# One diffusion step on one core: partial sums of the down projection kept in DRAM, some weight halves loaded by casting DMAs, and a new placement of the side work

## The chip, the cores and the metric

The kernel runs on one core of one Trainium2 chip, in one launch. The metric is the device time in microseconds (us). The program of before took 1320.09 us (median of three runs, 1320.08 to 1320.2).

## What is computed

One layer of a hybrid transformer acts on 128 context tokens and 128 latent tokens with the same fp32 weights (D = 2048, feed-forward width 8192):

```
m = silu(cond) @ w_ada + b_ada            # 6 vectors of 2048 per stream: shift, scale, gate, twice
h = rms_norm(x) * (1 + scale1) + shift1
p = h @ w_in                              # 8704 columns: q, k, v of mixers A and B, gate_A, gate_B
o_A = windowed attention (sink, rotary), o_B = neighbourhood attention (bias)
x = x + gate1 * ((sigmoid(gate_A) * (o_A @ w_br_a) + sigmoid(gate_B) * (o_B @ w_br_b)) @ w_out)
h2 = rms_norm(x) * (1 + scale2) + shift2
x = x + gate2 * (relu(h2 @ w_up) ** 2 @ w_down)
```

The two streams differ in `cond` and in the attention. Outputs are both streams and the new keys and values of the context.

## The kernel before

**Steps.** All big products run as 456 steps in a list (`wsteps`). A step is one 128x1024 fp32 weight tile (512 KB). SyncE loads it (`raw`), ScalarE copies it to fp32r (`wH`, through `copy`, L101), VectorE subtracts to get the rest (`wL`, L249), and TensorE does twelve 512-column matmuls: two k rows, two streams, and three products (high by high, low by high, high by low). Steps 0 to 135 are the input projection, 136 to 167 the branches, 168 to 199 the output projection, 200 to 215 the first two blocks of the up projection. Then for p = 1 to 7 come 16 steps of an up pair (216 to 231, 248 to 263, ...) and 16 of a down piece (232 to 247, ...); 440 to 455 are the last down piece.

**Order.** Nothing is scheduled by a tool: each engine's order is the order in which Python emits. `run` walks the steps. Before step i it emits the loads that are due up to i + `RUN[i]` (a load's due time is its step less 4), then the preparation (`prep_to`) of the steps up to i + `LOOK[i]`, then the step's matmuls, then what `at(i, ...)` has hung behind it. So a digit of `LOOK` moves a ScalarE and a VectorE instruction past their neighbours, and a digit of `RUN` moves loads past what else SyncE issues. `POST` gives three steps for each q/k unit: square sums (`qk_stat`, whose `rsqrt` runs on GpSimd), scaling (`qk_apply`, ScalarE and VectorE, which needs GpSimd's answer `rq`) and transposes (`qk_T`). `JOBS` gives five steps for each of eight attention jobs: scores, softmax, normalise, transposes, values. `DOTS*` place the modulation dot products on VectorE (`dot`, L1448, two of 1.2 us for each job).

**Low halves by DMA.** For the steps in `LO_DMA`, `lo_dma` has ScalarE write -`wH` (L255) and GpSimd issue an accumulating DMA of the fp32 weights onto it (L256), so VectorE does nothing.

**Up pairs.** `up_pair` treats a pair of 512-column blocks at eight k positions. At the positions in `FAST` it uses seven products in place of eight (a Winograd form): 21 matmuls in place of 24, with sums of weights made on VectorE and ScalarE (`prep_x`, `prep_y`). There are 34 such groups.

**Down pieces.** `down_unit(p, n)` multiplies 1024 of the 8192 hidden values into one of four 512-column blocks. The running sum of each block stays in SBUF (`dsum`, four of the 50 tiles of the pool `gen`). ScalarE copies it into two PSUM banks ahead of a unit (`seed`, `SEED_AT` = 3 steps before, or at the end of an up pair) and out again behind it.

**Modulation columns.** `mod_pair` takes two 128-column blocks (512 KB quarters `araw`, L308) at the steps in `ADA_AT`; `pair_mm` does the two blocks one after the other, 256 columns at a time in four 32-column groups of TensorE (L316). For the dot products the SiLU of `cond` is needed as a row over all partitions: `load_cond` broadcasts `crow`, `silu_cond` applies SiLU to the whole 128x1024 tile (ScalarE L1426, VectorE L1427) and GpSimd stores one row (L1429) for later use. This happens four times.

Of the kernel before, what the change touches and what calls it, by code (L numbers as in the profile page):

```python
# [51 lines left out]
LO_DMA = [50, 54, 56, 63, 77, 107, 129, 141, 145, 176, 184, 187, 188, 189, 203, 228, 233, 250, 286, 297, 360, 388, 392, 403, 447]  # L52
LO_AHEAD = 2

LOOK = "744424025212231324035524333325102425654224523344556654121016645555652437464478555443415652626353315000022636320000411134313532054023400446230326565645456443574337324421522555644666674052000205311111322534110323455554321045445111013410444324654734331001335565775443654453304436533423355423455542233213213545587654334232213213202440122544412433432313432443523324313211333435533333213331314344422557756822145342656433332302254541454475574464555546763333345544"
RUN = "788542236756223234111350006888532114464200022565595544354324444434399864356664356543323535443143130021224242014401314413432357530331035587886464765545676867644543555342013141268665576965588956265287998988511453877787785653022200123446553345324545104653232464345673321110102222521121211202355533232133432223443232410110000000011234344212022112531112752123301000112323643331133410100122454235566436675432012021222210010001154457832224556577677636445664422234"
CONST_AT = [83, 81]
XL_DMA = []
ADA_AT = [None, 4, 13, 22, 25]
XS_AT = {1: 3, 2: 24, 3: 34}  # L60
POST = {('kvA', 0): [81, 83, 89], ('qA', 0): [84, 84, 92], ('qA', 1): [86, 88, 92], ('kB', 0): [90, 94, 98], ('qB', 0): [94, 98, 104], ('kB', 1): [98, 101, 103], ('qB', 1): [102, 105, 107]}
JOBS = [[93, 94, 95, 100, 106], [93, 94, 98, 104, 106], [98, 98, 100, 106, 114], [101, 104, 107, 110, 111], [107, 107, 110, 115, 120], [109, 109, 111, 118, 121], [113, 114, 115, 126, 128], [116, 116, 119, 122, 124]]
# [3 lines left out]
DOTS = [44, 58, 61, 61, 62, 63, 65, 66, 66, 66, 69, 70, 71, 71, 72, 74, 76, 81, 84, 85, 89, 91, 94, 96, 96, 98, 100, 100, 101, 102, 102, 105, 107, 107, 107, 110, 110, 111, 113, 114, 115, 117, 117, 117, 120, 120, 120, 121, 121, 123, 123, 124, 127, 128, 128, 132, 132, 133, 133, 134, 135, 136, 141, 143, 144, 144, 149, 151, 151, 152, 157, 157, 157, 162, 163, 170, 172, 174, 174, 175, 176, 176, 178, 179, 179, 182, 183, 190]  # L66
DOTS2 = [224, 231, 231, 233, 235, 237, 238, 242, 245, 263, 265, 269, 275, 296, 299, 304, 309, 329, 331, 331, 333, 333, 353, 360, 362, 364, 366, 368, 382, 391, 394, 396]
STAT_AT = [-1, -1, 8, 16]
T_PAIR = [[9, 10], [6, 9], [8, 9], [8, 9], [10, 14], [10, 10], [11, 14]]
P_PAIR = [[5, 5], [2, 2], [2, 4], [6, 2], [4, 2], [4, 4], [6, 0]]  # L70
M_TE = (3,)
M_AT = [6, 6, 9]
# [7 lines left out]
def tile_hybrid_step(ctx: ExitStack, tc: tile.TileContext, a):  # L80
# [7 lines left out]

    act, dve, pe, pool, sync = nc.scalar, nc.vector, nc.tensor, nc.gpsimd, nc.sync
# [80 lines left out]

    r = SM(2, "r")
# [69 lines left out]
    def prep(st):  # L241
# [8 lines left out]
        st.pop("raw")  # L250
# [18 lines left out]

    by_dma = sorted(LO_DMA)  # L270

    def run():
        loads.sort(key=lambda x: x[:2])
        for st in wsteps:
# [6 lines left out]
            while by_dma and by_dma[0] < to + LO_AHEAD:  # L281
                prep_to(by_dma[0] - LO_AHEAD)
                lo_dma(wsteps[by_dma.pop(0)])
# [35 lines left out]
    def pair_mm(box, j, fb):  # L319
        for q in range(4):  # L320
            pair_mm_q(box, j, fb, q)
# [172 lines left out]
    def mod_pair(f):  # L494
# [3 lines left out]
        for j in range(2):  # L498
            load_at(i, lambda j=j: pair_load(box, 0, k0 + j))
            at(i, lambda j=j: pair_mm(box, j, k0 + j))  # L500
# [22 lines left out]
    def begin():  # L523
# [42 lines left out]
        mod_q(0, 3)  # L566
        x_scale(0, 0, 2)
# [61 lines left out]
    dp = ctx.enter_context(tc.tile_pool(name="dram", bufs=1, space=bass.MemoryType.DRAM))  # L629
# [584 lines left out]
    def up_pair(p):  # L1214
# [32 lines left out]
        for pos, is_fast in enumerate(kinds):  # L1247
# [16 lines left out]
            def prep_x(b=b, pos=pos):  # L1264
                b["XH"] = G("XH", F32R)
                copy(b["XH"], b["x"]["raw"])
                if 8 * p + pos in XL_DMA:
                    b["XL"] = G("XL", F32R)
                    minus_plus(b["XL"], b["XH"], b["x"]["src"])
# [28 lines left out]
            def mm_y(st, b=b, j=j, pos=pos, end=end):  # L1298
# [37 lines left out]
            for i, (nm, pf, mf) in enumerate((("x", prep_x, mm_x), ("y", prep_y, mm_y))):  # L1336
                add_step(a["w_upF"][p - 1, j, i], mf, key)
                b[nm] = wsteps[-1]
                wsteps[-1]["prep"] = pf

    dsum = {}
# [10 lines left out]
    def seed(p, n):  # L1352

        seeds[p, n] = [bank("acc", pacc) for _ in range(2)]
        for s in range(2):
            copy(seeds[p, n][s], dsum[n][:, s, :])
        if p == last:
            dsum.pop(n)

    def down_unit(p, n):  # L1360
        def evac(acc):
            if p == 0:
                dsum[n] = G(f"dsum{n}").rearrange("p (s n) -> p s n", s=2)
            if p == last:
                out_s(acc, n, range(2))
                return
            for s in range(2):
                copy(dsum[n][:, s, :], acc[s])
# [8 lines left out]
        if p and (n or p == last):  # L1377
# [4 lines left out]
        unit(a["w_down"], 512 * n, [4 * j for j in PIECES[p]], stat, evac, ("down", p, n), seeded if p else None)  # L1382
# [31 lines left out]
    silu_row = {}  # L1414

    def load_cond(h, tag):
        for s in range(2):
            cB[s, tag] = G(f"cB{s}")
            src = silu_row[s, h] if (s, h) in silu_row else a["crow"][s:s + 1, 1024 * h:1024 * h + 1024]
            sync.dma_start(cB[s, tag], src.partition_broadcast(P))  # L1420

    def silu_cond(h, s, tag):
        if (s, h) in silu_row:
            return
        t, c = G("sgB"), cB[s, tag]
        act.activation(t, c, AF.Sigmoid)  # L1426
        dve.tensor_tensor(c, c, t, op=OP.mult)  # L1427
        silu_row[s, h] = dp.tile([1, 1024], F32, name=f"silu{s}{h}")
        pool.dma_start(silu_row[s, h], c[0:1, :])  # L1429
# [52 lines left out]
    def dots(jobs, name):  # L1482
# [147 lines left out]
```

## Time and profile before

| | |
|---|---|
| median of three runs | 1320.09 us |
| the profiled execution | 1319.34 us, of it 1317.6 us from the first to the last instruction |
| mean granted TensorE clock | 0.999 |
| TensorE (PE) busy | 1300.7 us, 99% |
| VectorE (DVE) busy | 1149.5 us, 87% |
| ScalarE (ACT) busy | 925.8 us, 70% |
| GpSimd (POOL) busy | 62.9 us, 5% |
| DMA | 393.81 MB, 299 GB/s on average |

PEld is TensorE's weight load, SP is SyncE, L12 is line 12 of the kernel. The records of matmuls overlap, so that a busy TensorE says that work was queued; the idle time is the better guide, and where it lies.

### The profile page before, as it was taken

Reading aid. Unit: us, or ns where it says so; the run is one execution under the profiler, and the core shown is the slowest. Engines: PE = TensorE matmul, PEld = TensorE weight load, DVE = VectorE, ACT = ScalarE, POOL = GpSimd, SP = SyncE. Lnnn points to the kernel's source line nnn. Section 1 sums busy time; section 2 is a strip of 40 time slices with the busy share of each in tenths; the row PEclk is TensorE's granted clock in tenths of the full one; section 3 lists DMA queues with packets and bytes.
Section 4 is the critical chain, followed back from the end, with each engine's and each line's share of the span. In section 5 each row is a group of like instructions: output and inputs, shape, how many; then the busy total and the mean of one; then the engine's idle time right before and its main releaser. Section 6 shows DMA issues by size and latency. Waiting matters only on the chain.

```text
span 1317.6 us, 17782 instructions
## 1 busy us (share of the span) xinstructions
PE 1300.7 (99%) x6137; PEld 1056.9 (80%) x6137; DVE 1149.5 (87%) x1530; ACT 925.8 (70%) x1310; POOL 62.9 (5%) x71
## 2 busy tenths in 40 slices
PE   8999999999999999999999999999999999999998
PEld 4777888878777878888888888888888888888886
DVE  4569999999999999999779999897989998979753
ACT  5667766679866555755687867969678687796881
POOL 0000000241100000000000000000000000000000
PEclk9999999999999999999999999999999999999999
DMA  9999999887889999999498865888587696857692
GB/s 376 406 389 409 383 363 322 318 301 294 291 332 383 400 380 335 370 352 368 146 322 290 273 229 185 278 285 286 196 301 237 208 319 242 298 162 298 201 348 80
DMA packets 148394, 393.81 MB, mean 299 GB/s; under 512 B 51792, under 2 KB 52752, under 8 KB 148304
## 3 DMA queue, kind: packets, MB, share of 16 engines
q1 hardware_dynamic: 144016, 378.16, 78.4%
q0 software_dynamic: 4144, 14.44, 5.5%
q8 instruction: 48, 0.79, 0.2%
q14 instruction: 42, 0.34, 0.1%
q10 hardware_dynamic: 144, 0.08, 0.0%
HBM read 373.97 MB, written 8.70 MB: 290 GB/s over the span
## 4 chain that ended last, share of the span: by engine, by line
PE 63%; DVE 4%; issue 1%; DVEq 0%
PE acc L300 12%; PE acc L299 12%; PE acc L301 12%; PE Q L1225 6%; PE Q L1226 6%; PE Q L1224 6%; DVE wL L249 1%; DVE junk L1448 1%; DVE aT L1448 1%; PE Z L1225 1%; PE Z L1226 1%; PE Z L1224 1%; PE acc L1063 1%; PE acc L1044 1%; PE acc L1061 1%
## 5 line engine op out<-in xcount | busy, mean ns | idle before, releaser
L249 DVE TENSOR_TENSOR wL<-raw,wH 128x1024 fp32r<-128x1024 f32 x360 | 425.1, 1225 | 73.2 <-ACT wH L101 72.3
L101 ACT ACTIVATE wH<-raw 128x1024 fp32r<-128x1024 f32 (+1 forms) x391 | 388.6, 1044 | 71.9 <-PE acc L300 13.0
L1448 DVE SCALAR_TENSOR_TENSOR aT<-aT,cB 128x1024 f32<-128x1024 f32 x144 | 173.6, 1221 | 1.1
L1448 DVE SCALAR_TENSOR_TENSOR junk<-aT,cB 128x1024 bf16<-128x1024 f32 x144 | 173.9, 1224 | 0.0
L417 PE MATMUL acc<-wH,hH 128*128 128x512 f32 x276 | 109.1, 395 | 0.0
L419 PE MATMUL acc<-wH,hL 128*128 128x512 f32 x276 | 107.9, 391 | 0.0
L418 PE MATMUL acc<-wL,hH 128*128 128x512 f32 x276 | 107.9, 391 | 0.0
L101 ACT ACTIVATE uH<-raw 128x1024 fp32r<-128x1024 f32 x34 | 36.2, 1064 | 66.4 <-DVE raw L1286 60.7
L417 PEld LDWEIGHTS acc<-wH,hH 128*128 128x128 f32 x276 | 52.2, 189 | 13.1 <-issue 1.4
L419 PEld LDWEIGHTS acc<-wH,hL 128*128 128x128 f32 x276 | 52.1, 189 | 11.0
L418 PEld LDWEIGHTS acc<-wL,hH 128*128 128x128 f32 x276 | 52.3, 189 | 10.5
L101 ACT ACTIVATE tH<-t 128x1024 fp32r<-128x1024 f32 x34 | 36.0, 1059 | 29.8 <-DVE t L1279 28.8
L299 PE MATMUL acc<-wH,hH 128*128 128x512 f32 x128 | 52.2, 408 | 0.0
L300 PE MATMUL acc<-wL,hH 128*128 128x512 f32 x128 | 50.3, 393 | 1.7 <-DVE wL L249 1.7
L452 PE MATMUL acc<-wH,hH 128*128 128x512 f32 x128 | 50.5, 394 | 1.1 <-ACT acc L101 1.1
L453 PE MATMUL acc<-wL,hH 128*128 128x512 f32 x128 | 49.9, 390 | 0.3 <-DVE wL L249 0.3
L301 PE MATMUL acc<-wH,hL 128*128 128x512 f32 x128 | 50.0, 390 | 0.0
L454 PE MATMUL acc<-wH,hL 128*128 128x512 f32 x128 | 49.9, 390 | 0.0
L1289 DVE TENSOR_TENSOR uL<-raw,uH 128x1024 fp32r<-128x1024 f32 x34 | 41.7, 1226 | 1.2
L1279 DVE TENSOR_TENSOR t<-raw 128x1024 f32<-128x1024 f32 x34 | 41.5, 1219 | 1.3 <-PE Q L1225 1.3
L101 ACT ACTIVATE acc<-dsum 128x512 f32<-128x512 f32 x56 | 31.7, 589 | 14.7 <-DVE t L1010 7.3
L1288 DVE TENSOR_TENSOR tL<-t,tH 128x1024 fp32r<-128x1024 f32 x34 | 41.4, 1219 | 0.0
(643 smaller groups left out, 3353.7 us busy)
## 6 DMA issues: line engine op xcount, KB each, us to landing
raw<-in_w_in SPq DMA_DIRECT2D x133, 512.0 KB, 8.0
raw<-in_w_down SPq DMA_DIRECT2D x128, 512.0 KB, 5.9
aT<-in_w_adaT SPq DMA_DIRECT2D x80, 512.0 KB, 8.7
raw<-in_w_upF SPq DMA_DIRECT2D x68, 512.0 KB, 5.4
aT<-in_w_gT SPq DMA_DIRECT2D x64, 512.0 KB, 6.9
raw<-in_w_up SPq DMA_DIRECT2D x60, 512.0 KB, 6.1
araw<-in_w_pair SPq DMA_DIRECT2D x48, 512.0 KB, 9.5
raw<-in_w_out SPq DMA_DIRECT2D x32, 512.0 KB, 9.8
```

What stands on the lines that cost most here:

```text
L101: act.activation(out, in_, AF.Copy)
L249: dve.tensor_tensor(st["lo"], st["raw"], st["hi"].bitcast(F32), op=OP.subtract)
L299: pe.matmul(acc[tb], sh, wh[:, k, :], start=f, stop=False, skip_group_check=seeded)
L300: pe.matmul(acc[tb], sh, wl[:, k, :], start=False, stop=False, skip_group_check=seeded)
L301: pe.matmul(acc[tb], sl, wh[:, k, :], start=False, stop=l, skip_group_check=seeded)
L417: pe.matmul(acc[tb], sh, wh[:, k, :], start=opened[u] and k == 0, stop=False, skip_group_check=skip)
L418: pe.matmul(acc[tb], sh, wl[:, k, :], start=False, stop=False, skip_group_check=skip)
L419: pe.matmul(acc[tb], sl, wh[:, k, :], start=False, stop=last and k == 1, skip_group_check=skip)
L1224: pe.matmul(acc, stat[0], hi, start=f, stop=False)
L1225: pe.matmul(acc, stat[0], lo, start=False, stop=False)
L1226: pe.matmul(acc, stat[1], hi, start=False, stop=l)
L1448: dve.scalar_tensor_tensor(out, box["raw"], 1.0, cB[s, tag], op0=OP.mult, op1=OP.mult, accum_out=dst[:, s, fb:fb + 1])
```

## The change

- **Down sums.** `down_unit` evacuates each partial sum into a tile of its own; the first piece is stored to DRAM (`dmem`), pieces 1 to 6 are added there by GpSimd's accumulating DMA. Only the last piece is seeded: `sum_back` loads the sum 8 steps before the unit (`SUM_BACK`), `seed` copies it in 3 steps before.
- **Casting loads.** For the 15 steps in `HI_DMA` GpSimd loads the weights straight into `wH` as fp32r. Where the step is in `LO_DMA` too (12 of them), no `raw` is loaded. `LO_DMA` grows from 25 to 33 steps, all eight new ones at 218 or later. `XL_DMA` = [22, 63] makes the low part of two fast tiles by an accumulating DMA.
- **SiLU rows.** `silu_rows` makes them once, in `begin`, from the columns: a 32-column multiply, a transpose, a copy and a 16 KB store. `load_cond` always reads that; `silu_cond` and `crow` go.
- **Modulation pairs.** `wide_mm` takes two blocks at once, 512 columns for each k, from a layout `w_pair2` with the same bytes.
- **35 groups** in `FAST` (5, 4, 5, 6, 5, 5, 5 for p = 1 to 7; before 4, 5, 5, 5, 5, 5, 5).
- **Placement.** `LOOK` and `RUN` change by a few digits in about 160 and 150 places, `POST`, `JOBS`, `DOTS*`, `STAT_AT`, `T_PAIR`, `P_PAIR`, `M_AT`, `BACK` and others by a little.

```diff
-DOTS1 = [9, 11, 14, 19, 22, 22, ...
+DOTS1 = [10, 11, 16, 22, 24, 24, ...
-FAST = {1: (0, 2, 5, 7), 2: (0, 4, 5, 6, 7), 3: (0, 2, 4, 5, 7), 4: (0, 2, 4, 5, 7), ...
+FAST = {1: (0, 2, 3, 5, 7), 2: (0, 3, 6, 7), 3: (0, 2, 4, 5, 7), 4: (0, 2, 3, 4, 5, 7), ...
-QK_ACT = [('qB', 1)]
+QK_ACT = [('kB', 0), ('qB', 1)]
-BACK = 9
+BACK = 7
-GATE_BACK = 2
+GATE_BACK = 1
-LO_DMA = [..., 145, 176, 184, 187, 188, 189, 203, 228, 233, 250, 286, 297, 360, 388, 392, 403, 447]
+LO_DMA = [..., 145, 177, 184, 187, 188, 189, 203, 218, 219, 225, 228, 233, 250, 251, 296, 297, 331, 337, 360, 388, 392, 394, 399, 437, 447]
+XL_DMA = [22, 63]
+HI_DMA = [219, 225, 228, 229, 250, 251, 296, 331, 337, 394, 399, 404, 437, 438, 447]
+SUM_BACK = 8
-POST = {('kvA', 0): [81, 83, 89], ('qA', 0): [84, 84, 92], ('qA', 1): [86, 88, 92], ..., ('qB', 1): [102, 105, 107]}
+POST = {('kvA', 0): [81, 83, 89], ('qA', 0): [84, 87, 92], ('qA', 1): [85, 88, 92], ..., ('qB', 1): [102, 106, 107]}
-JOBS = [[93, 94, 95, 100, 106], [93, ...
+JOBS = [[94, 94, 95, 100, 106], [93, ...
# LOOK[84] 4 to 5, [85] 1 to 0, [86] 5 to 4, [98] 5 to 6, [99..102] 0 to 1, [132] 4 to 5, [133] 0 to 1, ...
+    silu_mem = dp.tile([2 * KC, P], F32, name="silu")
+    silu_row = silu_mem.rearrange("(s k) f -> s (k f)", s=2)
+    def silu_rows():
+        t = SM(32, "silu")
+        dve.tensor_tensor(t, cols[:, 0:32], sg, op=OP.mult)
+        ps = bank("ps_sl")
+        pe.transpose(ps[0:2 * KC, 0:P], t, ident)
+        row = sp.tile([P, 512], F32, name="srow", tag="S", bufs=2)[0:2 * KC, 0:P]
+        copy(row, ps[0:2 * KC, 0:P])
+        sync.dma_start(silu_mem, row)
         def load():
             if "raw" not in st:
+                if st["i"] in HI_DMA:
+                    st["hi"] = G("XH" if "x" in st else "wH", F32R)
+                    pool.dma_start(st["hi"], src)
+                    if st["i"] in LO_DMA:
+                        return
                 st["raw"] = G("raw")
                 sync.dma_start(st["raw"], src)
     def lo_dma(st):
-        prep_hi(st)
+        if "early" in st:
+            st.pop("early")()
+            return
+        if "hi" not in st:
+            prep_hi(st)
+    def wide_mm(box, half):
+        if half == 0:
+            box["ps"] = bank("ps_ada")
+        for q in range(4 * half, 4 * half + 4):
+            raw = box.pop(q).rearrange("p (k n) -> p k n", k=2)
+            for k in range(2):
+                c = 32 * (2 * (q % 2) + k)
+                pe.matmul(box["ps"][c:c + 32, 0:512], cpad[:, 2 * q + k, :], raw[:, k, :],
+                          start=q < 2, stop=q > 5, tile_position=(0, c))
         mod_q(0, 3)
+        silu_rows()
         x_scale(0, 0, 2)
-                    if p > 1:
-                        seed(p - 1, 0)
+    def sum_back(n):
+        t = G(f"dsum{n}")
+        sync.dma_start(t, dmem[n])
+        dsum[n] = t.rearrange("p (s n) -> p s n", s=2)
     def down_unit(p, n):
         def evac(acc):
-            if p == 0:
-                dsum[n] = G(f"dsum{n}").rearrange("p (s n) -> p s n", s=2)
             if p == last:
                 out_s(acc, n, range(2))
                 return
+            t = G(f"dpart{n}")
             for s in range(2):
-                copy(dsum[n][:, s, :], acc[s])
+                copy(t[:, 512 * s:512 * s + 512], acc[s])
+            if p == 0:
+                dmem[n] = dp.tile([P, 1024], F32, name=f"dm{n}")
+                sync.dma_start(dmem[n], t)
+            else:
+                pool.dma_start(dmem[n], t, accum_op=OP.add)
-        if p and (n or p == last):
+        if p == last:
+            i = len(wsteps) - SUM_BACK
+            at(i, lambda: sum_back(n))
             at(len(wsteps) - SEED_AT, lambda: seed(p, n))
```

## Rows read from the trace of the kernel before

**Rows 1.** The page: busy time of each engine, and the DMA queues.

```profile
PE 1300.7 (99%) x6137; PEld 1056.9 (80%) x6137; DVE 1149.5 (87%) x1530; ACT 925.8 (70%) x1310; POOL 62.9 (5%) x71
...
q1 hardware_dynamic: 144016, 378.16, 78.4%
q0 software_dynamic: 4144, 14.44, 5.5%
```

**Rows 2.** Busy time by stretch: us, each engine (instructions), granted clock, DMA share, GB/s.

```profile
41.00:45.00 4.00, 4.00 (x18) 2.91 (x11) 1.23 (x1) 1.66 (x2) 0.00 (x0) 0.57 1.02 382
...
300.00:350.00 50.00, 46.87 (x250) 39.28 (x249) 45.62 (x79) 47.53 (x156) 12.66 (x11) 1.00 0.80 289
...
500.00:550.00 50.00, 50.00 (x222) 41.27 (x221) 49.79 (x69) 34.49 (x31) 0.00 (x0) 1.00 0.99 340
...
1000.00:1100.00 100.00, 100.00 (x443) 82.84 (x442) 91.73 (x105) 77.56 (x87) 0.86 (x1) 1.00 0.74 259
...
480.00:1313.00 833.00, 832.75 (x3693) 688.96 (x3691) 726.00 (x876) 597.73 (x679) 15.48 (x20) 1.00 0.79 268
```

**Rows 3.** Waits of TensorE from 250 to 500 us: total, times, longest.

```profile
PE acc L300 <- DVE wL L249: 2.1, 3, 1.1
PE ps_S L807 <- ACT T_qA L766: 1.7, 1, 1.7
PE acc L452 <- ACT acc L101: 1.1, 1, 1.1
PE ps_o L861 <- ACT probT L101: 0.8, 1, 0.8
...
PE acc L453 <- DVE wL L249: 0.3, 1, 0.3
```

**Rows 4.** Waits of VectorE from 250 to 500 us.

```profile
DVE wL L249 <- ACT wH L101: 6.8, 6, 2.8
...
DVE u_qA L735 <- POOL rq L145: 0.9, 2, 0.4
```

**Rows 5.** Time line of TensorE: modulation pairs, and transposes of a query unit.

```profile
40.65 0.79 PE L316 MATMUL ps_ada<-araw,rt 128*32 128x256 f32 x8 [0.63 <-DMA araw<-in_w_pair]
...
67.97 3.66 PE L316 MATMUL ps_ada<-araw,rt 128*32 128x256 f32 x64
...
298.94 1.91 PE L760 MATMUL ps_qT<-ident,u_qA 128*128 128x128 f32 x16
```

**Rows 6.** Groups of instructions from 700 to 1300 us: busy, mean ns | idle before.

```profile
L101 ACT ACTIVATE wH<-raw 128x1024 fp32r<-128x1024 f32 x165 | 163.8, 1048 | 6.7 <-DMA raw<-in_w_down 4.6 <-PE Z L1226 1.5 <-PE acc L300 0.7
...
L101 ACT ACTIVATE acc<-dsum 128x512 f32<-128x512 f32 x56 | 31.7, 589 | 14.7 <-DVE t L1010 7.3 <-DVE up L1324 7.1
...
L249 DVE TENSOR_TENSOR wL<-raw,wH 128x1024 fp32r<-128x1024 f32 x156 | 183.3, 1220 | 36.7 <-ACT wH L101 36.2 <-issue 0.3
...
L1286 DVE TENSOR_TENSOR raw<-raw 128x512 f32<-128x512 f32 x32 | 21.9, 685 | 0.0
```

**Rows 7.** Time line of ScalarE and GpSimd around the query units: start, us, what.

```profile
278.71 2.48 POOL L145 TENSOR_TENSOR rq<-rs,pw 128x8 f32<-128x8 f32 x1
...
281.23 1.28 ACT L730 ACTIVATE u_qA<-u_qA,rq 128x128 f32<-128x128 f32 x4 [4.53 <-POOL rq L145]
...
302.63 2.01 ACT L101 ACTIVATE wH<-raw 128x1024 fp32r<-128x1024 f32 x2
...
304.52 0.69 ACT L766 ACTIVATE T_qA<-ps_qT,cols 128x512 f32<-128x512 f32 x1
```

**Rows 8.** Time line of TensorE at two of its waits for low halves.

```profile
341.79 0.50 PE L300 MATMUL acc<-wL,hH 128*128 128x512 f32 x1 [1.13 <-DVE wL L249]
...
462.60 0.50 PE L300 MATMUL acc<-wL,oHA 128*128 128x512 f32 x1 [0.47 <-DVE wL L249]
```

**Rows 9.** Accumulating DMAs (L256): landing of all; and issues of the page.

```profile
DMA to landing us min/median/max: 5.4/8.6/12.0
...
raw<-in_w_down SPq DMA_DIRECT2D x128, 512.0 KB, 5.9
```

More of the change, by code (lines that the diff above doesn't have):

```diff
@@ L268, in prep_to @@
             prep_next[0] += 1
-    by_dma = sorted(LO_DMA)
     def run():
         loads.sort(key=lambda x: x[:2])
+        by_dma = sorted(set(LO_DMA) | {st["i"] for st in wsteps if "early" in st})
         for st in wsteps:
@@ L282, in run @@
                 prep_to(by_dma[0] - LO_AHEAD)
+                while loads and loads[0][0] <= by_dma[0] - LOAD:
+                    loads.pop(0)[2]()
                 lo_dma(wsteps[by_dma.pop(0)])
@@ L317, in pair_mm_q, with wide_load @@
                       start=j == 0 and q == 0, stop=(j == 1 or alone) and q == 3, tile_position=(0, 32 * k))
-    def pair_mm(box, j, fb):
-        for q in range(4):
-            pair_mm_q(box, j, fb, q)
+    def wide_load(box, nsub, f, half):
+        for q in range(4 * half, 4 * half + 4):
+            box[q] = G("araw")
+            sync.dma_start(box[q], a["w_pair2"][nsub, f][:, 1024 * q:1024 * q + 1024])
+    def wide_mm(box, half):
+        if half == 0:
+            box["ps"] = bank("ps_ada")
+        for q in range(4 * half, 4 * half + 4):
+            raw = box.pop(q).rearrange("p (k n) -> p k n", k=2)
[3 more added lines that the diff above has]
+                          start=q < 2, stop=q > 5, tile_position=(0, c))
     def ada_evac(box, n=512):
@@ L1262, in up_pair, with high_x, early_x, prep_x @@
             b = {}
[L1264 to L1269, printed above, removed]
+            def high_x(b=b):
+                b["XH"] = b["x"].pop("hi", None)
+                if b["XH"] is None:
+                    b["XH"] = G("XH", F32R)
+                    copy(b["XH"], b["x"]["raw"])
+            def early_x(b=b):
+                high_x(b)
+                b["XL"] = G("XL", F32R)
+                minus_plus(b["XL"], b["XH"], b["x"]["src"])
+            def prep_x(b=b):
+                if "XH" not in b:
+                    high_x(b)
             def prep_y(b=b, pos=pos):
@@ L1338, in up_pair @@
                 b[nm] = wsteps[-1]
+                if nm == "x":
+                    wsteps[-1]["x"] = True
+                    if 8 * p + pos in XL_DMA:
+                        wsteps[-1]["early"] = early_x
+                else:
+                    assert wsteps[-1]["i"] not in HI_DMA
                 wsteps[-1]["prep"] = pf
-    dsum = {}
+    dsum, dmem = {}, {}
     last = len(PIECES) - 1
@@ L1354, in seed @@
         seeds[p, n] = [bank("acc", pacc) for _ in range(2)]
+        t = dsum.pop(n)
         for s in range(2):
-            copy(seeds[p, n][s], dsum[n][:, s, :])
-        if p == last:
-            dsum.pop(n)
+            copy(seeds[p, n][s], t[:, s, :])
+    def sum_back(n):
+        t = G(f"dsum{n}")
+        sync.dma_start(t, dmem[n])
+        dsum[n] = t.rearrange("p (s n) -> p s n", s=2)
     def down_unit(p, n):
         def evac(acc):
-            if p == 0:
-                dsum[n] = G(f"dsum{n}").rearrange("p (s n) -> p s n", s=2)
             if p == last:
@@ L1376, in seeded @@
             return seeds.pop((p, n))
-        if p and (n or p == last):
+        if p == last:
+            i = len(wsteps) - SUM_BACK
+            assert i > end_of(("down", last - 1, n))
+            at(i, lambda: sum_back(n))
             at(len(wsteps) - SEED_AT, lambda: seed(p, n))
@@ L1381, in down_unit @@
             return
-        unit(a["w_down"], 512 * n, [4 * j for j in PIECES[p]], stat, evac, ("down", p, n), seeded if p else None)
+        unit(a["w_down"], 512 * n, [4 * j for j in PIECES[p]], stat, evac, ("down", p, n), seeded if p == last else None)
     for n in PIECES[0]:
@@ L1412, in tile_hybrid_step @@
     cB = {}
-    silu_row = {}
     def load_cond(h, tag):
@@ L1591, in _layout @@
         w = ada[:, p * D:(p + 2) * D].reshape(KC, P, 2, KC, P)
-        pairs.append(w.transpose(3, 1, 0, 2, 4).reshape(KC, P, KC * 2 * P))
-    out["w_pair"] = np.stack(pairs)
+        pairs.append(w.transpose(3, 1, 0, 2, 4))
+    out["w_pair"] = pairs[0][None, 0:2].reshape(1, 2, P, KC * 2 * P)
+    out["w_pair2"] = np.stack([w.reshape(KC // 2, 2, P, KC, 2 * P).transpose(0, 2, 3, 1, 4).reshape(KC // 2, P, KC * 4 * P)
+                               for w in pairs])
     def rows_of(part, f0):
```

60 lines of the change are left out of this document (24 added, 36 removed).

## The prediction

> **What bounds the kernel now.** Begin with the page: TensorE is busy 1300.7 of the span [rows 1], 1317.6 us, so only its idle time and its count of matmuls can give anything. Then the busy time by stretch: from 480 to 1313 us TensorE is busy 832.75 of 833 us, at the full granted clock, 2.4 GHz [rows 2]. Whatever is taken off ScalarE, VectorE or SyncE behind 480 us buys nothing by itself; it can only do harm where it makes weights late. Third, the waits of TensorE from 250 to 500 us: seven, 2.1 + 1.7 + 1.1 + 0.8 + 0.3 = 6.0 us [rows 3]. They lie where queries and keys are normalised and the attention is run; from 300 to 350 us TensorE loses 3.13 of 50 us, and ScalarE is at 47.53 [rows 2]. Last, who is late: VectorE is busy 49.79 of 50 us from 500 to 550 us [rows 2], and from 250 to 500 us it waits 6.8 us for high halves that ScalarE had not yet copied and 0.9 for GpSimd's `rq` [rows 4]. The two engines that prepare wait for one another there, and TensorE for both. The first 45 us are set by DMA: the last quarter of the first modulation pair comes 0.63 us late [rows 5], and behind such gaps the granted clock is 0.57 from 41 to 45 us [rows 2], mostly the lower level, 1.2 GHz.
>
> **The change, part by part.** The sum is made against the profiled execution, 1319.34 us (the span and 1.7 around it); the median of the runs is 0.75 us above it, which I add at the end.
>
> *35 groups.* One group more saves three matmuls (21 for 24). 443 matmuls fill 100 us [rows 2], so one takes 0.226 us: **-0.7 us**. The group costs VectorE four passes of 1.22 and three of 0.69, 6.9 us, where two plain steps cost 2 x 1.22 [rows 6]: +4.5 us, for an engine with 8.3 of 100 us to spare from 1000 to 1100 us [rows 2], from which eight new low halves by DMA and two `XL` take 10 x 1.22 away. It stays hidden; without that cover it would cost 4.5 us.
>
> *The seeds and the casting loads.* 48 of 56 copies of 589 ns leave ScalarE [rows 6], 28 us; 15 casting loads take 15 x 1.05 more off it, and ten new negations (L255) put 10 x 1.05 back. ScalarE gains 33 us over 600 us in which no TensorE instruction waits for it: **0**. The matmul that opened on a seeded bank now overwrites it, at the same 0.226 us.
>
> *The queries* (`POST`). The square sums and the scaling of the first query unit both hung behind step 84. GpSimd takes 2.48 us for `rq` alone, and ScalarE stood 4.53 us at the head of its queue for it, until 281.23 [rows 7]. Queued behind were a value unit's evacuation, weight copies and the seed of the next gate unit; TensorE's 1.1 us at `acc L452` and the 0.3 us behind it come from there [rows 3]. Three steps between the two (84 to 87, and 85 to 88 for the second unit) are 36 matmuls, 8 us, and cover GpSimd. At 302.63 ScalarE was still behind: two weight copies stood ahead of the transposed queries at 304.52 [rows 7], for which the scores waited 1.7 us [rows 3]. With 4.53 us given back that wait falls too, although the second job still asks at step 93. A matmul behind a wait lasts 0.50 us [rows 8] where 0.226 is the pace; so each wait costs some 0.2 us more than this view counts. So 1.1 + 0.3 + 1.7 + 0.6, less 0.4 left over: **-3.3 us** (bounds 0 and -3.7).
>
> *Earlier preparation* (`LOOK`). At 341.79 and 462.60 us TensorE waited 1.13 and 0.47 us for a `wL` [rows 8]. The preparation of step 104 was emitted at step 103 and now at 98; that of step 137 at 135, now at 132. With the restarts the bounds are 0 and -2.2. But VectorE does no less for being asked earlier, what stood there moves back by 1.22 us, and it is full up to 550 us. I take **-1.2 us**. The third wait for `wL` and that for `probT` (0.5 and 0.8) have no edit that reaches them: 0.
>
> *What is late next.* TensorE comes to 500 us some 4.5 us earlier, and VectorE must have gained as much. It gains the 0.9 us of `rq`, 0.69 by the key unit handed to ScalarE (nearest row L1286) [rows 6], and what falls of its 6.8 us for ScalarE's copies [rows 4]; I take half, 3.4, so 5.0. That is barely enough, and I set **+0.6 us** for one more wait (bounds 0 and +3).
>
> *The prologue.* `silu_rows` puts a multiply, a transpose and a copy ahead of the first modulation evacuation, about 0.5 us (two transpose records at 0.12 [rows 5] and a small copy, bound 0.59 [rows 6]). TensorE is later by that when it comes to the first pair, where three quarters are late anyway, the last by 0.63 us [rows 5]: hidden, **0**; without the cover +0.5. SyncE issues the 16 KB store behind loads that DMA still has to finish, so what is queued behind it loses nothing. Four SiLU passes leave ScalarE and VectorE before 140 us, where no wait is due to them: 0. Bounds for these 45 us are -1.6 (the dip of the clock goes: eight matmuls at half speed [rows 2]) and +1.6 (it comes twice).
>
> *The modulation pairs.* 64 records of 256 columns in 3.66 us become 32 of 512. 16 records of 128 columns over the whole array take 1.91 us, 0.12 each, and four of 256, side by side, 0.23 [rows 5]: time goes with columns, so **0**. If time went by records, each of five pairs would give 1.8 us; if the four column groups no longer ran side by side, each would cost 3.7 us more. Four consecutive matmuls still go to four groups, so both lie at the edge of the range or past it.
>
> *The DMA.* Here a cover is used up. The software queue takes 5.5% of the span for 14.44 MB, 5.0 us a MB, 2.6 us for 512 KB; the plain queue 78.4% for 378.16 MB, 1.4 us for 512 KB [rows 1]. Behind 690 us come 24 sums, 15 casting loads and 10 more low halves (49 x 2.6 = 127 us) and 8 plain transfers of sums (11 us); 12 plain loads go (17 us). Over 610 us that is +0.20 of share on 0.74 [rows 2]. At 0.94 loads still keep up: at 0.99, from 500 to 550 us, TensorE was busy throughout [rows 2]. So **0**; the price without cover stands below.
>
> In the Trainium skill, "DMA: Bandwidth & Descriptors", section "Anatomy of one DMA — SWDGE (gpsimd) path", a GpSimd transfer costs 2.0 us and its bytes at 436 GB/s, with no other figure for one that accumulates. By that 512 KB would hold the DMA engines 1.2 us, and the share would be an estimated 0.83; the rows, twice that and from accumulating transfers, decide for me.
>
> *New waits.* `sum_back` stands on SyncE until the last addition has landed. It comes five steps behind the addition's issue, 60 matmuls, 13.6 us; accumulating DMAs land in 5.4 to 12.0 us [rows 9]. If it were late, loads for later steps would be held behind it. A casting load waits on GpSimd for a free tile, with additions queued behind it that are wanted only a piece later.
>
> Sum: -0.7 - 3.3 - 1.2 + 0.6 = -4.6, so 1314.7 for a profiled execution and **1315.5 us** for the median.
>
> **The rivals.**
>
> *VectorE is the bound.* Waits taken from TensorE only push it against a VectorE with no idle time from 500 us on. Then only VectorE's sure savings count, 0.9 + 0.7, and the group: -2.3, **1317.8 us**. For it: 49.79 of 50 [rows 2]. Against: its 6.8 us of waits for ScalarE [rows 4], whose cause is edited.
>
> *The query waits stay* (the change does not do what it says). The second job still asks at step 93, weight copies still stand ahead, and the waits only change names: -0.7 - 1.2, **1318.2 us**. Against it: the 4.53 us at 281 are plainly a wait for GpSimd [rows 7].
>
> *DMA runs full in the down pieces* (slower). An addition into DRAM reads and writes there, and no row shows one; its cost lies between a plain 1.4 us and, I allow, twice 2.6. Without the sums the share is 0.74 + 0.10; 24 sums over 500 us bring it to 1.03 at 4.0 us each. From there TensorE waits for weights by the overrun: at 4.4 us each, 0.02 x 500 = 10 us, **1325 us**. For it: accumulating transfers land in 8.6 us where weights land in 5.9 [rows 9]. Against: only the upper part of the bounds reaches it, and the tiles that `dsum` held are free for earlier loads.
>
> *All goes.* 6.0 us of waits with 2 of restart, the clock's 1.6 and the group: about -10, **1310 us**.
>
> **How the numbers follow.** Forecast 0.60; VectorE 0.14; waits stay 0.10; DMA, or a like lateness of weights behind 600 us, 0.11; all goes 0.05. This kernel's measurement can tell 0.2%, 2.6 us. Faster needs less than 1317.45: the forecast and the last, 0.65, and 0.01 of VectorE's case, 0.66. Within 0.2%: the rest of VectorE's, most of the second, 0.21. Slower: 0.13. The forecast's own range is 1313 to 1317.4; with the other cases it is 1311 to 1321.5.
>
> **What would show it.** The scaling at step 87 without a ScalarE wait for `rq`; no TensorE wait for `acc L452` or T_qA; none for `wL` at steps 104 and 137; VectorE's waits for `wH` from 250 to 500 us near 3 us; additions and casting loads landing within 12 us; a DMA share near 0.94 behind 800 us, with TensorE idle for nothing there. I am wrong if TensorE waits more than 2 us behind 480 us, if new waits between 300 and 500 us come to more than 4 us, or if the pairs at L316 take over 4 us.

## The result, and the profile after

The changed kernel takes 1326.88 us (median of 20 runs, 1321.74 to 1331.87), the kernel before 1320.20 (20 runs measured with them, 1318.84 to 1322.36): ratio 1.0049, 95% interval 1.0035 to 1.0062, **slower by 0.35 to 0.62%**. The forecast was 1315.5 us, with a chance of 0.66 on faster. The runs of the changed kernel ("after") also scatter over 10 us, those of the kernel before over 3.5.

The profiled execution of after took 1325.82 us, with a span of 1324.1; before 1319.34 and 1317.6. The page's rows for the engines and the DMA queues, beside [rows 1]:

```profile
PE 1303.6 (98%) x5974; PEld 1051.4 (79%) x5975; DVE 1137.6 (86%) x1521; ACT 897.9 (68%) x1260; POOL 98.8 (7%) x116
...
q1 hardware_dynamic: 143488, 376.08, 77.5%
q0 software_dynamic: 11072, 40.11, 14.5%
```

ScalarE lost 28 us of work (33 forecast), and the share of the software queue went from 5.5 to 14.5%. Busy time by stretch (us, engines, granted clock, DMA share, GB/s), beside [rows 2]:

```profile
680.00:725.00 45.00, 43.22 (x183) 34.97 (x182) 39.10 (x44) 31.52 (x35) 2.61 (x3) 0.96 1.07 351
721.00:724.60 3.60, 3.60 (x9) 2.83 (x10) 3.28 (x3) 2.06 (x3) 0.00 (x0) 0.53 1.05 345
480.00:1313.00 833.00, 827.45 (x3655) 682.75 (x3654) 717.08 (x868) 569.39 (x627) 53.27 (x69) 1.00 0.92 294
1000.00:1100.00 100.00, 100.00 (x442) 82.78 (x442) 93.61 (x111) 71.38 (x76) 6.03 (x7) 1.00 0.91 291
```

From 480 to 1313 us TensorE was idle for 0.25 us before and is idle for 5.55 now, where the forecast had nothing. Its waits there:

```profile
PE ps_h L1137 <- DVE h2f L1129: 1.3, 1, 1.3
PE acc L326 <- ACT acc L104: 1.3, 1, 1.3
PE Q L1264 <- ACT uH L104: 1.0, 1, 1.0
PE Q L1265 <- DVE uL L1337: 1.0, 2, 0.8
PE acc L327 <- DMA wL<-in_w_down: 1.0, 1, 1.0
```

To see where time goes I set the first matmul of each stretch in one time line against the same in the other. After is 1.6 us ahead at 613 us (the front works), 0.1 ahead at 637 (the second norm cost 1.5), 3.2 behind at 723 (the first up pair, which should have gained 0.7 by its fifth group, lost 3.3: a loss of 4.0), 3.9 behind at 1269 and 6.8 at TensorE's last matmul (the last down piece cost 2.9).

The 4.0 us of the first pair are more than its two waits, 1.03 and 0.76 us. Right behind the second the granted clock was 0.53 from 721.0 to 724.6 us, mostly the lower level, 1.2 GHz: matmuls came 0.43 us apart in place of 0.23, which makes about 1.6 us. Before has no such dip behind 45 us.

### The profile page after: what moved, and what is told of

Read it like the earlier page. It is cut to its first block, busy times and chain, and to the rows that moved or that the text cites. A ratio compares the mean times of both kernels' runs of the same rounds, so it can differ in the third digit from the quotient of the medians.

```text
span 1324.1 us, 17519 instructions
## 1 busy us (share of the span) xinstructions
PE 1303.6 (98%) x5974; PEld 1051.4 (79%) x5975; DVE 1137.6 (86%) x1521; ACT 897.9 (68%) x1260; POOL 98.8 (7%) x116
## 3 DMA queue, kind: packets, MB, share of 16 engines
q0 software_dynamic: 11072, 40.11, 14.5%
## 4 chain that ended last, share of the span: by engine, by line
PE 44%; DMA 7%; DVE 3%; issue 1%; ACT 1%; SPq 0%; DVEq 0%; ACTq 0%
PE acc L326 8%; PE acc L327 8%; PE acc L328 8%; PE Q L1265 5%; PE Q L1266 5%; PE Q L1264 5%; DMA dsum<-dm 2%; DMA raw<-in_w_out 2%; DMA pTa<-pla 1%; DMA raw<-in_w_upF 1%; DMA raw<-in_w_up 1%; PE Z L1266 1%; PE Z L1265 1%; PE Z L1264 1%; DVE junk L1500 0%
## 5 line engine op out<-in xcount | busy, mean ns | idle before, releaser
L270 DVE TENSOR_TENSOR wL<-raw,wH 128x1024 fp32r<-128x1024 f32 x350 | 414.7, 1226 | 94.8 <-ACT wH L104 94.3
L104 ACT ACTIVATE wH<-raw 128x1024 fp32r<-128x1024 f32 (+1 forms) x374 | 373.7, 1044 | 88.7 <-DMA raw<-in_w_down 15.1
L458 PEld LDWEIGHTS acc<-wL,hH 128*128 128x128 f32 x276 | 51.8, 188 | 10.8 <-DVE wL L270 0.4
L1379 ACT ACTIVATE up<-up 128x1024 f32<-128x1024 f32 x28 | 29.7, 1062 | 30.5 <-DVE up L1372 30.0
L104 ACT ACTIVATE dpart<-acc 128x512 f32<-128x512 f32 x56 | 31.6, 590 | 20.4 <-PE acc L328 19.3
L104 ACT ACTIVATE fTa<-pTa 128x2048 uint16<-128x2048 uint16 x16 | 40.5, 2533 | 6.1 <-DMA pTa<-pla 6.1
```

The lines of the kernel that those rows point to most:

```text
L104: act.activation(out, in_, AF.Copy)
L270: dve.tensor_tensor(st["lo"], st["raw"], st["hi"].bitcast(F32), op=OP.subtract)
L458: pe.matmul(acc[tb], sh, wl[:, k, :], start=False, stop=False, skip_group_check=skip)
```

## The experiments

Each was run together with the kernel before on one chip; beside runs 1 to 4, 5 to 8, 9 to 12 and 13 to 16 that kernel took 1320.31, 1320.14, 1320.15 and 1320.44 us. "Pair 1" is what the first up pair took more than in the kernel before, in us and in the profiled run alone, with the three matmuls that a fifth group saves added back. "Flip" is the second transposing load of that pair (`up_flip`, L970): how long it held SyncE, and how long after its issue it landed, in us.

| kernel | median us (runs), range | ratio, 95% | pair 1 | flip |
|---|---|---|---|---|
| after | 1326.88 (20), 1321.7–1331.9 | 1.0035–1.0062 | 4.0 | 12.3, 16.6 |
| 1 after, sums in SBUF | 1329.71 (6), 1320.7–1336.7 | 1.0046–1.0105 | 9.3 | 12.9, 25.6 |
| 2 after, no casting loads | 1329.42 (6), 1327.7–1333.0 | 1.0063–1.0091 | 4.9 | 9.0, 13.8 |
| 3 after, `sum_back` by GpSimd | 1328.67 (6), 1324.5–1332.4 | 1.0047–1.0084 | 13.1 | 12.6, 26.0 |
| 4 front half only | **1317.50** (11), 1316.9–1318.5 | 0.9971–0.9988 | 0 | 1.9, 4.3 |
| 5 after, no added DMA | 1324.97 (5), 1322.6–1325.5 | 1.0023–1.0047 | 4.6 | 6.0, 8.0 |
| 6 front + sums in DRAM | 1331.61 (6), 1325.8–1340.5 | 1.0070–1.0120 | 0 | 2.8, 4.4 |
| 7 front + casting loads, low halves | 1318.40 (11), 1317.1–1320.2 | 0.9979–0.9996 | 0 | 7.5, 9.6 |
| 8 after, seven transfers less | 1324.48 (5), 1322.4–1326.2 | 1.0021–1.0047 | 3.0 | 5.4, 7.4 |
| 9 as 5, 34 groups | 1321.10 (11), 1319.4–1323.2 | 1.0001–1.0018 | 0 | 5.1, 7.1 |
| 10 front + fifth group in pair 1 | 1322.06 (11), 1321.1–1322.7 | 1.0003–1.0021 | 3.9 | 3.0, 4.4 |
| 11 front + sixth group in pair 4 | 1320.63 (11), 1319.7–1321.6 | 0.9996–1.0014 | 0 | 3.0, 4.4 |
| 12 after, 34 groups | 1332.76 (4), 1331.7–1336.2 | 1.0089–1.0120 | 11.3 | 15.8, 25.2 |
| 13 as 12 and 8 together | 1322.22 (12), 1320.2–1328.8 | 1.0006–1.0029 | 0 | 6.2, 8.2 |
| 14 as 6, sums not loaded back | 1329.82 (6), 1326.5–1331.2 | 1.0055–1.0081 | 0 | 1.9, 4.3 |
| 15 front, new order to step 239 | 1319.04 (11), 1318.2–1320.5 | 0.9977–0.9995 | 0 | 7.3, 9.4 |
| 16 front, old query steps | 1320.39 (11), 1319.8–1321.4 | 0.9990–1.0008 | 0 | 2.2, 4.3 |

**Runs 1 to 4: one part undone, and the front half alone.** 1 (`evac` copies to `dsum`, every piece seeded):

```diff
-            pool.dma_start(dmem[n], t, accum_op=OP.add)
+            for s in range(2):
+                copy(dsum[n][:, s, :], acc[s])
```

> The changed kernel with the down sums back in SBUF, seeded by copies on ScalarE; everything else stays, the casting loads too. Theory A (the added transfers fill DMA, so that loads are late everywhere behind 640 us): the DMA share behind 800 us falls from about 0.92 to about 0.80, the 7 us lost behind 640 us go nearly all, about 1320 us. Theory B (SyncE stands at sum_back and at transposes that wait for earlier loads): only the loss in the last down piece goes, 2.7 us, where SyncE stood 10.1 us for the addition; the 3.3 us of the second norm and the first pair stay; about 1324 us. Theory C (the new order of the preparing steps costs time by itself, DMA has no part in it): within 1 us of the changed kernel, 1326.

2: `HI_DMA = []`.

> The changed kernel without casting loads: ScalarE makes those 15 high parts from the landed weights, as the others. Theory A: 15 x 2.6 us of DMA time less over 600 us is a share 0.06 lower, so one to two of the 7 us come back, about 1325 us. Theory B: GpSimd's queue is shorter, SyncE's as before; no change, 1326 to 1327. Theory C: ScalarE has 15 copies of 1.05 us more in steps that were placed without them; up to 1 us slower, 1327 to 1328.

3:

```diff
-        sync.dma_start(t, dmem[n])
+        pool.dma_start(t, dmem[n])
```

> The changed kernel with sum_back, the load of a down sum from DRAM, issued by GpSimd in place of SyncE; nothing else is changed. Theory B: SyncE no longer stands 10.1 us for the addition before the last piece, its weight loads come earlier, and TensorE's 0.96 and 1.26 us of waits with their restarts go: 2 to 3 us less, about 1324. GpSimd stands there instead, with additions and casting loads behind it; if those are wanted, part of it comes back. Theory A: the same bytes in the same time, so no change, 1326 to 1327. Theory C: no change either.

4: from step 176 on `LOOK` and `RUN` of before, and its `FAST`, `LO_DMA`, `DOTS`, `DOTS2`, `STAT_AT`, `T_PAIR`, `P_PAIR`, `M_AT`, `BACK`, `GATE_BACK`; `HI_DMA = []`, `XL_DMA = []`; sums as in 1.

> The first half of the change alone: SiLU rows once, the modulation products on two blocks, the query work three steps later, a key unit's half by ScalarE, and the new order of preparing steps up to step 175; from there on the order, the groups (34), the low halves by DMA and the down sums in SBUF are those of the kernel before. By the prediction's terms for queries and earlier preparation this is 3.9 us faster than before, 1316.3. By the trace after, where 2.4 us were gained by step 104 and 1.6 kept by the end of the output projection, it is 1.6 us faster, 1318.6, and all theories of the loss place that loss behind this point. Should the loss show here too, it comes from the first half.

The front half gains 2.8 us, and nothing else undone helps: without the sums, without the castings or with `sum_back` on GpSimd (1 to 3) the medians are above every time that I had set, and within the scatter of after's runs. Theory A in its wide form and B as the main cause fell. After and runs 1 to 3 all lost most in the first pair, so I looked at the transposing load there. In after, and in run 4:

```profile
L970 SPq DMA_TRANSPOSE pTa<-pla x1: 12288/12288/12288, 690.5 to 690.5; - x1
...
DMA to landing us min/median/max: 16.6/16.6/16.6
```

```profile
L970 SPq DMA_TRANSPOSE pTa<-pla x1: 1939/1939/1939, 686.4 to 686.4; - x1
...
DMA to landing us min/median/max: 4.3/4.3/4.3
```

SyncE is held until what it issued earlier has landed: in after to 702.8 us, the last earlier load landing at 700.5; of the 19 such loads in after, those with a load of SyncE's still 2 us or more from landing release SyncE between 0.25 us before and 2.3 us after that landing. Some end with a GpSimd transfer instead: in run 7 the one at 1247.29 us, with no load of SyncE's under way, held SyncE for 4.6 us, until 0.2 us before a casting load landed. The longer the queue, the longer SyncE stands. The DMA from 684 to 700 us, in after and in run 4 (packets, MB, share of 16 engines):

```profile
DMA packets 1769, 6.29 MB, mean 393 GB/s; under 512 B 236, under 2 KB 236, under 8 KB 1769
...
q1 hardware_dynamic: 1377, 4.88, 78.0%
q0 software_dynamic: 392, 1.41, 29.1%
```

```profile
DMA packets 2608, 2.47 MB, mean 155 GB/s; under 512 B 2136, under 2 KB 2136, under 8 KB 2606
...
q1 hardware_dynamic: 2606, 2.45, 52.7%
```

The same stretch moves 6.29 MB in place of 2.47. In front of the transposing load went six of the seven software-queue transfers of steps 218 to 229, the last of which landed at 690.55 us, and the plain loads beside them, some of which the new `RUN` asks for earlier. The seventh, a low half, was issued at 694.1 us, while SyncE stood.

**Runs 5 to 8: added transfers, sums, castings, each by itself.** 5: as 1 and 2, with `LO_DMA` of before and `XL_DMA = []`. 6: run 4 with DRAM sums as in after. 7: run 4 with `HI_DMA` and `LO_DMA` of after. 8:

```diff
-LO_DMA = [..., 203, 218, 219, 225, 228, 233, ...
+LO_DMA = [..., 203, 228, 233, ...
-HI_DMA = [219, 225, 228, 229, 250, ...
+HI_DMA = [250, ...
```

> The changed kernel without any of its added software-queue transfers: down sums in SBUF, no casting loads, the low halves by DMA of the kernel before; kept are the new order of preparing steps, the 35 groups and the front half. After the first four runs the sums alone and the castings alone explain nothing (1329.7 and 1329.4 without them), and most of the loss comes when a transposing load of the first pair, behind a queue of some 15 us, holds SyncE 9 to 13 us. Theory A' (the castings, low halves and sums together make that queue): without all of them the loss goes, 1316.5 to 1318. Theory C (the new order asks for loads in bunches, whatever they carry): 1323 to 1330 still, with the transposing load at 690 us holding SyncE over 6 us.

> The fast first half (1317.5) with one part added: down sums added in DRAM; order, 34 groups and low halves from step 176 on as before. If additions themselves cost (theory A), DMA share rises by about 0.1 behind 800 us and the time by 3 us or more, 1320.5. Theory B: SyncE stands at sum_back for the addition in the last piece, 2 to 3 us, 1320. Theory C: the old order has room, within 1 us of 1317.5.

> The fast first half (1317.5) with one part added: the 15 casting loads and the ten more low halves by DMA of the change; sums in SBUF, order and 34 groups from step 176 on as before. Theory A' (these transfers make the queue in front of the transposing load of the first pair): that load holds SyncE over 6 us and lands over 10 us after its issue, 1320 to 1325. Theory C (the order makes it): the load at 687 us holds SyncE about 2 to 3 us, as in the kernel before, and the time is within 1 us of 1317.5.

> The changed kernel without seven software-queue transfers of the first pair: the casting loads of steps 219, 225, 228 and 229 and the low halves of steps 218, 219 and 225 are made by ScalarE and VectorE again. Seven times about 2.6 us is 18 us of DMA time between 656 and 700 us. Theory A' in its local form: the transposing load at 690 us holds SyncE 3 to 5 us in place of 12.3, the first pair's 3.3 us of loss goes, about 1323. Theory C: 1326 or more, the transposing load still held over 8 us; and 4 + 3 more passes on ScalarE and VectorE may add to it.

The flip holds SyncE for 1.9 us in the front half, 7.5 with the castings and the low halves by DMA (7), 6.0 with the new order alone (5), 12.3 with both (after): both theories were partly right, and the two add. But a flip that lands 7 to 10 us after its issue harms nothing (runs 7, 9, 13, 15), and runs 5 and 8 lost 4.6 and 3.0 us in pair 1 all the same. So pair 1 had a second cause. These transfers cost 0.9 us on the front half, though the intervals of runs 4 and 7 overlap. The sums cost 14 us there; no term of mine allowed that. In the new order they are far cheaper: run 13, with the sums and most of the other added transfers, is 1.1 us slower than run 9 without any, and run 8 is no slower than run 5.

**Runs 9 to 12: the fifth group.** 9: run 5 with `FAST[1] = (0, 2, 5, 7)`. 10: run 4 with `FAST[1] = (0, 2, 3, 5, 7)`. 11: run 4 with `FAST[4] = (0, 2, 3, 4, 5, 7)`. 12: after with `FAST[1] = (0, 2, 5, 7)`.

> The kernel without added transfers (1325.0, 35 groups in the new order) with the first pair back at four groups, (0, 2, 5, 7): 34 groups in all. In its trace VectorE works without a pause from 702 us, the last group's `uL` comes at 720.05 where the fast first half has it at 716.86, and TensorE loses 3.9 us and the 0.7 that the group saves. Theory D (the fifth group costs VectorE 4.5 us in the one pair that has none to spare): the first pair loses nothing, TensorE runs 0.7 longer and 4.6 shorter, 1321. Theory C (the order of the preparing steps, not the group): the wait for uH and uL stays or moves, 1324 to 1326.

> The fast first half (1317.5), the old order behind it, with one part added: a fifth group in the first pair, at position 3. Theory D: VectorE is late in the first pair by about 4 us less what slack it had, the time is 1320 to 1322, and the waits are for uH and uL of the last group. Theory C: the old order carries it, 1316.8 to 1318.

> The fast first half (1317.5) with the 35th group put into the fourth pair, which VectorE enters with 8 of 100 us to spare, in place of the first: (0, 2, 3, 4, 5, 7). Theory D: the group costs nothing there and saves three matmuls, 0.7 us: 1316.8. If VectorE lacks room there too: 1318 to 1320. It would be the fastest of all versions if the first holds.

> The whole change, only with the first pair at four groups, (0, 2, 5, 7). Theory D: of the 6.7 us lost against before, the first pair's loss of 3.3 us goes and the group's 0.7 is paid, 1324; the last piece's loss and the scatter stay. Theory A'' (the queue of added transfers before the transposing load is what makes the first pair late): no gain, 1326 to 1330, with that load still holding SyncE over 8 us.

Theory D holds both ways in pair 1: taken out, the group gives 3.9 us back (5 to 9); put in, it costs 4.6 (4 to 10). VectorE's first and last pass of the pair's last group, in run 4 and in run 10 (start, us, what):

```profile
709.31 1.22 DVE L1327 TENSOR_TENSOR t<-raw 128x1024 f32<-128x1024 f32 x1
...
715.63 1.23 DVE L1337 TENSOR_TENSOR uL<-raw,uH 128x1024 fp32r<-128x1024 f32 x1
```

```profile
712.87 1.22 DVE L1327 TENSOR_TENSOR t<-raw 128x1024 f32<-128x1024 f32 x1
...
719.23 1.22 DVE L1337 TENSOR_TENSOR uL<-raw,uH 128x1024 fp32r<-128x1024 f32 x1
```

The group's passes put the last group 3.6 us back, and TensorE waits in run 10, as after does 0.4 us later, for its `uH` and `uL`. Ahead of these run 10 also waits for a low half by DMA: ScalarE's negation for it came at 700.26 us, in run 4 at 696.76.

```profile
712.37 0.50 PE L1265 MATMUL Q<-wL,h23H 128*128 128x512 f32 x1 [1.44 <-DMA wL<-in_w_up]
...
719.25 0.50 PE L1264 MATMUL Q<-uH,sH 128*128 128x512 f32 x1 [0.67 <-ACT uH L104]
...
720.51 0.50 PE L1265 MATMUL Q<-uL,sH 128*128 128x512 f32 x1 [0.76 <-DVE uL L1337]
```

D failed in pair 4 of the old order: there too the 35th group costs 3.1 us (run 11: waits for XL, uL and a seed). In the new order a sixth group in pair 4 came free: in after the lag falls there from 3.8 to 3.1 us, by the 0.7 of three matmuls. And run 12 shows that the flip is a cause of its own: without the fifth group, but with the flip landing 25 us after its issue, pair 1 loses 11.3 us.

```profile
L970 SPq DMA_TRANSPOSE pTa<-pla x1: 15800/15800/15800, 690.7 to 690.7; - x1
...
  ACT fTa L104: 11.2, 1
```

The wait of 11.2 us is ScalarE's. In order behind it stand the copies for the pair's last group and, through them, VectorE and TensorE, which waits for `XL`, `uH` and `uL` (2.80, 0.81, 0.47 us in the time line). A wait of 1.98 us at 708 us came earlier, for a low half whose accumulating DMA took 13.8 us to land. Together that is 6.1 of the 11.3 us; most of the rest is the clock, which was granted at 0.51, mostly the lower level, from 709.0 to 712.5 and from 726 to 733 us, behind these waits.

**Runs 13 to 16: both together, the way back, the order, the front.** 13: the edits of 8 and 12. 14: run 6 without `sum_back` and without seeds in the last piece. 15: run 4 with `LOOK` and `RUN` of after up to step 239, `STAT_AT`, `M_AT` of after. 16: run 4 with `POST`, `JOBS`, `QK_ACT` of before.

> The whole change with both suspects taken out of the first pair: four groups there, (0, 2, 5, 7), and without the seven software-queue transfers of steps 218 to 229. With the transfers alone gone (four steps up) the pair still lost 2.3 us and the group's 0.7; with the group alone gone it lost 11.3. If the two together are the pair's whole loss, it is 0 there, the transposing load at 687 us holds SyncE under 6 us, and what is left against the kernel before is the last pieces' 2 to 3 us and the norm's 1 to 3 us, less the front's 1.6: 1321 to 1323. If there is a third cause, the pair still loses over 2 us and the time is 1324 or more.

> The fast first half with down sums in DRAM (1331.6), of which the last piece's part is left out: the sums are not loaded back and no bank of the last piece is seeded, so the output holds the last piece's products alone; all 28 additions and stores stay. If the way back (addition, then load, then copy into the bank) is what holds up the last piece, its 8.4 us go and the 3.6 us lost from 767 to 1269 us stay: 1322 to 1324. If the additions' DMA time makes weights late, the last piece still loses 3 us or more: 1326 and up.

> The fast first half with the new order kept up to step 239, the end of the first pair, four groups in it, and no added transfers; behind it the old order. With the new order the norm lost 0.3 us at 630 and the first pair nothing, where the fast first half lost 0.6 at 630. If what was lost behind 890 us in that kernel came only from seeds in an order placed without them, this is 0.3 to 0.6 us faster than the fast first half, 1317.0; if the change of orders in the middle costs, 1318 to 1320.

> The fast first half (1317.5) with the query, key and job steps of the kernel before; the earlier preparation, the SiLU rows and the wide modulation products stay. By the prediction's terms the queries are worth 3.3 of 4.5 us and this is slower than the first half by that: 1320.8. By the trace, where waits of 1.1 for the bank and 0.8 for T_qA went, it is 2 us slower: 1319.5. If the earlier preparation carries the gain: 1317.5 to 1318.

13 came as expected, but for the flip's 6.2 us where I had under 6: pair 1 loses nothing, and 4.7 us are back. What TensorE still waits for behind 480 us there:

```profile
PE acc L326 <- ACT acc L104: 1.6, 1, 1.6
PE ps_h L1137 <- DVE h2f L1129: 1.0, 1, 1.0
PE Q L1265 <- DVE uL L1337: 0.2, 1, 0.2
```

14 suggests that the way back is the lesser part of what the sums cost: without it the median falls from 1331.6 to 1329.8 only. In the profiled runs the loss behind 1226 us, in the last two pieces, fell from 8.4 to 1.8 us, but 4.5 were lost from 1142 to 1226 us, where run 6 lost 1.2; with runs that scatter by 5 to 15 us one profile does not settle the shares. 15 costs 1.5 us against the front half, so it is not the 1317.0 of late seeds alone. Its profile, the slowest of its 11 runs, has 1.3 us of wait for the second norm's `h2f` at 631 us; runs 5 and 9 have the same order there and wait 0.4 us and not at all, so whether the order brings that wait is open. 16: the query steps are worth 2.9 us.

## Why the prediction was wrong

*35 groups*, the step that failed first. I wrote "it stays hidden; without that cover it would cost 4.5 us", and took the cover from 1000 to 1100 us [rows 2]. No group is added there: pair 1 goes from four to five, pair 2 from five to four, pair 4 from five to six. And such an average hides where VectorE is idle. In the kernel before, while TensorE is in pair 1, in pair 4 and in the down piece behind that:

```profile
682.50:723.30 40.80, 40.80 (x181) 33.78 (x181) 36.96 (x43) 30.93 (x34) 1.80 (x2) 1.00 0.90 276
934.40:974.50 40.10, 40.10 (x179) 33.21 (x178) 39.34 (x44) 24.44 (x29) 0.00 (x0) 1.00 0.73 259
974.50:1018.00 43.50, 43.50 (x194) 36.03 (x193) 37.83 (x47) 38.05 (x42) 0.00 (x0) 1.00 0.78 258
```

VectorE is idle for 5.7 us in that piece, 0.8 in pair 4, and 3.8 in pair 1, where it also does the second norm's planes and the gate dots. In run 4 nearly all of that idle time is waits for ScalarE (3.6 us), and run 10 has them too (3.9), so the group's passes don't fill them. The group cost 3.9 to 4.6 us net (5 to 9, 4 to 10); my price without cover was 4.5 less the 0.7 saved.

*The DMA*, which failed in kind. The share came out about as I had it (0.91 from 1000 to 1100 us, 0.94 forecast), and from 767 to 1100 us TensorE waits for nothing. But I asked whether the mean leaves room, not what stands behind a full queue at one place. The transposing load of 690 us holds SyncE until the queue before it is empty: 12.3 us where it was 3.1 before. My rival "DMA runs full in the down pieces" had the time nearly right, 1325, and the place wrong. In after's profiled run the flip landed after 16.6 us and the 4.0 us of pair 1 can be the fifth group's alone; where it landed after 25 or 26 (runs 1, 3, 12) the pair lost 9 to 13 us. That this is what makes after's runs scatter up to 1331.9 is likely but not shown: only one of them has a trace.

*The price of a wait.* I added 0.2 us to each wait. Where the clock fell behind a wait, that cost far more: about 1.6 us in after's pair 1 and, by what its waits leave of 11.3, about 4 in run 12's. Run 10, with waits of 1.44, 0.67 and 0.76 us in the pair, kept the full clock and lost 3.9.

*New waits.* "It comes five steps behind the addition's issue, 60 matmuls, 13.6 us" counted TensorE's steps. SyncE runs ahead of TensorE and stood at `sum_back` 0.8 us after the addition was issued (1244.01 us; it landed after 10.8); behind it came another transposing load. SyncE from 1243 us in after, and TensorE in the last piece:

```profile
1243.96 0.82 SPq L244 DMA_DIRECT2D raw<-in_w_down  x2
1254.90 0.33 SPq L1414 DMA_DIRECT2D dsum<-dm  x1
1255.33 8.10 SPq L970 DMA_TRANSPOSE pTa<-pla  x1
```

```profile
1293.39 0.50 PE L327 MATMUL acc<-wL,a15H 128*128 128x512 f32 x1 [0.96 <-DMA wL<-in_w_down]
...
1297.46 0.50 PE L326 MATMUL acc<-wH,a14H 128*128 128x512 f32 x1 [1.26 <-ACT acc L104]
```

SyncE stands 10.1 us at `sum_back` and 8.1 at the load, and weights and seed of the last piece are late by 1.0 and 1.3 us. Moving `sum_back` to GpSimd (3) left 0.6 of the last piece's loss in its profile, but the median shows no gain.

*The queries*: right in the main. Forecast 3.3, measured 2.9 (16 against 4); no ScalarE wait for `rq` is left, and `acc` of the gate unit isn't waited for, but the scores still wait 0.9 us for T_qA. What TensorE waits for from 250 to 500 us in after, beside [rows 3]:

```profile
PE ps_o L901 <- ACT probT L104: 1.2, 1, 1.2
PE ps_S L847 <- ACT T_qA L104: 0.9, 1, 0.9
PE ps_PT L894 <- ACT T_qB L806: 0.9, 1, 0.9
PE ps_qT L800 <- ACT T_kB L104: 0.9, 1, 0.9
...
PE acc L327 <- DVE wL L270: 0.6, 1, 0.6
```

*Earlier preparation*: its waits for `wL` fell from 2.1 to 0.6, but T_kB and T_qB are waited for by 1.8 us now. (Of that, T_qB had 0.3 before, which my list of seven waits left out, and the wait for T_kB is gone in run 16, so it seems to come with the query steps.) With the old query steps the rest of the front gives nothing (1320.39 against 1320.44): not -1.2 but 0. *What is late next* came at 630 us, at the second norm, 1.5 us for the 0.6 that I had set; in the front half alone it is 0.6. The whole front is worth 2.8 us where I had 3.9.

*The new order* behind step 175 I had not costed at all. With 34 groups and no added transfers it is 3.6 us slower than the old one (9 against 4). With the sums in SBUF its seeds are late (0.9 and 0.2 us at 975 and 923 us); but with the sums out, as it is meant to run (13), it still stands 4.7 us behind the front half. Where most of the 3.6 us goes is open: the profile of run 9 is 1.5 us under its median.

So the 9.4 us from the front half to after are 3.6 for the new order, 1.1 for the sums and most of the other added transfers in it (9 to 13), and 4.7 for the fifth group and the seven transfers in pair 1 (13 to after).

*Seeds and casting loads*: 0 forecast, 0.9 by run 7. Casting loads took up to 13.7 us to land, those of pair 1, where I had set 12 as a sign. *Modulation pairs*: 32 records of 512 columns in 3.64 us, 64 of 256 took 3.66 [rows 5]: right. *The prologue*: the dip of the clock from 41 to 45 us is gone (granted 1.00 for 0.57, behind a wait of 0.23 us for 0.63). After is 0.6 us ahead at 54 us, and at 239 us 0.3 of it is left.

The best version is run 4, 1317.50: 2.8 us faster than before, 9 faster than after.

## What to carry to other kernels

Ask for the cover where the work is put, not where the engine has most to spare: a 35th group, added to the old order, cost 4.6 us in one pair and 3.1 in another. Before adding transfers look for instructions that wait for a queue to empty (a transposing load, a load that waits for an addition) and count the queue in front of each; a mean DMA share under 1 says nothing of them. A wait put on an engine that runs ahead is to be dated by that engine's time line. And price a wait by the granted clock behind it too, not by its length alone.

## What the hardware showed

A transposing load lands 4.3 us after its issue on a nearly idle queue (run 4), and holds SyncE until the loads issued before it have landed. The Trainium skill, "Advanced Engine Details and Errata", section "X-Bar Transpose (TRN2)", says that such transfers are as fast as regular ones; the 4.3 us agree, as two plain loads land after 4.4 in that stretch of run 4. With 6.29 MB moved from 684 to 700 us, in after, SyncE stood 12.3 us and the load landed after 16.6. In run 12 it took 9.4 us more to land after SyncE was free, against 4.4 in after; from 702 to 717 us the DMA engines there moved little at a high share, with two accumulating low halves in flight, which landed late as well (13.8 and 17.8 us):

```profile
DMA packets 2148, 1.79 MB, mean 119 GB/s; under 512 B 1822, under 2 KB 1822, under 8 KB 2147
...
q1 hardware_dynamic: 1973, 1.16, 80.4%
q0 software_dynamic: 174, 0.62, 35.4%
```

Whether it is the small packets of the transposing load or the additions that slow the other was not tried and stays open, as does most of what makes additions into DRAM cost 14 us in the old order.
